# Differential attention: values projected two heads at a time straight into token rows

## The chip, the cores and the metric

The kernel runs on one core of a Trainium2 chip. The metric is the device time of one execution in microseconds (us), and the number to compare is the median of several runs. A core has five engines that work side by side, each with its own queue of instructions: PE (TensorE, matrix products; its weight loads are listed as PEld), DVE (VectorE), ACT (ScalarE), POOL (GpSimd) and SP (SyncE, which here issues most DMAs). Matmuls write into PSUM, a small memory of eight banks; the other operands live in SBUF. DMAs move data between SBUF and HBM.

## What is computed

The reference is an encoder trunk of two layers over 512 tokens of width 1024. In each layer the normalised input `h` goes through one wide projection `h @ w_in[l]`, whose columns feed three token mixers (MLA, windowed attention, differential attention) and three gates per channel; the merged result goes through `w_out`. The part that matters here is the differential attention: 4 heads, each with two score maps of dimension 64 and one value of dimension 128.

```
qc, kc, vc, zc = columns of h @ w_in[l]          # 512 columns each: 4 heads x 128
q, k = qc, kc as (S, 4 heads, 2, 64);  v = vc as (S, 4 heads, 128)
s = q . k / 8 + bias[head]                       # two maps per head, 512 x 512
p = softmax(s)
a = p[0] - lam * p[1]
o = rms_norm(a @ v, g_sub) * (1 - lam_init)
o_c = (o * silu(zc)) @ w_o_diff[l]
```

## The kernel before

**Precision by splitting.** A product of two float32 operands is made from three matmuls in the type fp32r: each operand is split into a high part (an ACT copy that rounds) and a low part (a DVE subtract), and `mm3` (lines 86 to 89) adds up high x high, high x low and low x high in one PSUM bank. The input of the layer is held transposed and split, in `hh` and `hl`: 128 channels in the partitions, 8 blocks `k` of channels, 512 tokens along the free dimension.

**Projections.** `wunit` (line 100) fetches a block of weights of 128 x 1024 elements (512 KB) into a buffer `wr` by a DMA on SP and splits it into `wh` (ACT, line 81) and `wl` (DVE, line 84). There are 2 buffers `wr` and 3 each of `wh` and `wl` (line 61). These steps have a high priority in the schedule, so they run ahead as far as buffers allow. `proj_T` (line 451) takes one unit, 128 columns with all 8 blocks `k`, and makes 24 matmuls: the weights are loaded into the array and the 512 tokens stream past. The result is 128 columns x 512 tokens, that is transposed, in a PSUM bank of the kind `dn`, of which there are 2. The other banks are `sc` (2, scores), `tr` (2, transposes), `av` (1) and `pj` (1).

**Order.** A scheduler lays out every engine's queue when the program is built. It takes the order of the program text as priority and lets later work start early where operands and buffers are ready. `tc.high_priority` moves a block forward. So independent projections fill TensorE while the softmax of a head runs on DVE, ACT and POOL.

**Differential attention** (line 924). `diff_qkv` (line 904) prepares a head: `stack_q` projects q, `proj_T` with `stack_k` projects k, and the value is projected by a third `proj_T`. The values are needed with tokens in the partitions, so `v_transposed` (line 805) copies the projection from PSUM to SBUF on ACT (buffer `tf`), transposes its four blocks of 128 x 128 on TensorE against the identity into the bank `pj` (line 810), and then ACT copies the high part (line 920) and DVE subtracts the low part (line 921) into a `big` buffer `vt` of 128 x 2 x 512. `first(hd)` makes the scores and the softmax of a head (lines 928 to 954). `second(hd, pr)` transposes the probabilities block by block (line 691) and multiplies them with the values (line 962), then normalises. The main loop (lines 982 to 996) prepares heads 0 and 1, starts `first(0)`, and then for each head runs: z's projection and its silu, one step of the merge of the windowed attention (`fill`), `first` of the next head, `second` of this head, and `diff_qkv` of the head after the next. `gates_late` and `gate_rows` (lines 505 and 280) follow behind the attention, then the merge of its output. `bg_step` advances unrelated work for later (modulation rows).

**The windowed attention** (line 839) matters as a comparison: its score matmuls (lines 865 and 866) stream 256 or 384 columns instead of 512. It uses `v_transposed` once a layer, too, and keeps it.

Of the kernel before, what the change touches and what calls it, by code (L numbers as in the profile page):

```python
# [12 lines left out]
F32R = mybir.dt.float32r  # L13
# [4 lines left out]
P = 128  # L18
S = 512
D = 1024  # L20
KT = D // P
NT = S // P
# [13 lines left out]
C_VC = 3232  # L36
# [14 lines left out]
def hybrid_kernel(ctx, tc, x, c, w_ada, b_ada, g_pre, g_post, w_in, g_q, w_uq, g_kv, w_ukv,  # L51
# [11 lines left out]
    def T(tag, shape, dt=F32, bufs=None):  # L63
        count[0] += 1
        return sb.tile(shape, dt, tag=tag, name=f"{tag}_{count[0]}",
                       bufs=bufs or BUFS.get(tag, 1))
# [6 lines left out]
    def Q(tag):  # L73
        count[0] += 1
        return ps.tile([P, S], F32, tag=tag, name=f"ps_{tag}_{count[0]}", bufs=PB[tag])

    def f(ap):
        return ap.bitcast(F32)

    def act_copy(out_, in_, scale=1.0):  # L80
        return act.activation(out=out_, in_=in_, func=AF.Copy, scale=scale)  # L81

    def sub(out_, a, b, eng=None):
        return (eng or dve).tensor_tensor(out=out_, in0=a, in1=b, op=ALU.subtract)  # L84

    def mm3(o, ah, al, bh, bl, start, stop):
        pe.matmul(o, ah, bh, start=start, stop=False)  # L87
        pe.matmul(o, ah, bl, start=False, stop=False)  # L88
        pe.matmul(o, al, bh, start=False, stop=stop)  # L89
# [3 lines left out]
    @contextmanager  # L93
    def behind(*ins):
        with ExitStack() as es:
            for i in ins or fence:
                es.enter_context(tc.issue_after(i.ins))
            yield

    def wunit(parts, big=False):  # L100
        raw = T("wr", [P, 1024])
        h = T("big" if big else "wh", [P, 1024], F32R)
        lw = T("big" if big else "wl", [P, 1024], F32R)
        n = parts[-1][1]
        with tc.high_priority(offset=WOFF[0]):
            for lo, hi, src, shp in parts:
                dst = raw[:, lo:hi]
                if shp:
                    dst = dst.rearrange("p (a b) -> p a b", a=shp)
                sp.dma_start(out=dst, in_=src)  # L110
            with behind():
                act_copy(h[:, :n], raw[:, :n])
                sub(lw[:, :n], raw[:, :n], f(h[:, :n]))
        return h, lw
# [160 lines left out]
    def bg_step(n=1):  # L275
        for _ in range(n):
            if bg and next(bg[0], bg) is bg:
                bg.clear()
# [172 lines left out]
    def proj_T(l, col, hh, hl):  # L451
        wh, wl = wunit([(0, 1024, w_in[l][:, col:col + P].rearrange("(k p) c -> p k c", p=P), KT)])
        acc = Q("dn")
        for k in range(KT):
            mm3(acc, wh[:, k * P:(k + 1) * P], wl[:, k * P:(k + 1) * P], hh[:, k], hl[:, k],
                k == 0, k == KT - 1)
        return acc
# [340 lines left out]
    def stack_k(src, i, kh):  # L798
        hi = slice(i * 64, i * 64 + 64)
        lo = slice(64 - i * 64, 128 - i * 64)  # L800
        act_copy(kh[hi], src[hi])
        dve.tensor_copy(out=kh[lo], in_=f(kh[hi]))
        return kh

    def v_transposed(vp):
        vf = T("tf", [P, S])
        act_copy(vf, vp)
        tr = Q("pj")
        for t in range(NT):
            pe.transpose(tr[:, t * P:(t + 1) * P], vf[:, t * P:(t + 1) * P], ident)  # L810
        return tr
# [89 lines left out]
        pipelined(first, second, 2 * NT)  # L901
        return o_all

    def diff_qkv(l, hd, hh, hl):
        bg_step()
        qq = stack_q(l, C_QC + hd * P, hh, hl)
        bg_step()
        kh = [T("op", [P, S], F32R) for _ in range(2)]
        kl = [T("op", [P, S], F32R) for _ in range(2)]
        ka = proj_T(l, C_KC + hd * P, hh, hl)  # L910
        for i in range(2):
            stack_k(ka, i, kh[i])
        for i in range(2):
            hi = slice(i * 64, i * 64 + 64)
            lo = slice(64 - i * 64, 128 - i * 64)
            sub(kl[i][hi], ka[hi], f(kh[i][hi]))
            dve.tensor_copy(out=kl[i][lo], in_=f(kl[i][hi]))
        vt = T("big", [P, 2, S], F32R)
        tr = v_transposed(proj_T(l, C_VC + hd * P, hh, hl))
        act_copy(vt[:, 0], tr)  # L920
        sub(vt[:, 1], tr, f(vt[:, 0]))
        return qq, kh, kl, vt

    def diff_attention(l, hh, hl, fill):
        o_all = []
        ops = {}

        def first(hd):
            qq, kh, kl, vt = ops[hd]
            b = T("x5", [P, 896])  # L930
            sp.dma_start(out=b, in_=skewed(bias_d[hd], 1023, 896))
            pr = T("p", [P, NT, S])
            for t in range(NT):
                ts_ = slice(t * P, (t + 1) * P)
                mx, nm, sm, rr = (stat(2) for _ in range(4))
                pc = [pr[:, t], T("ta", [P, S])]
                for i in range(2):
                    s = Q("sc")
                    pe.matmul(s, qq[i][:, ts_], kh[i], start=True, stop=False)  # L939
                    pe.matmul(s, qq[i][:, ts_], kl[i], start=False, stop=True)  # L940
                    dve.tensor_tensor_reduce(out=pc[i], in0=s, in1=b[:, 384 - t * P:896 - t * P],
                                             scale=1.0, scalar=-3.0e38, op0=ALU.add, op1=ALU.max,
                                             accum_out=mx[:, i:i + 1])
                    dve.tensor_scalar(out=nm[:, i:i + 1], in0=mx[:, i:i + 1], scalar1=-1.0,
                                      scalar2=None, op0=ALU.mult)
                    act.activation(out=pc[i], in_=pc[i], func=AF.Exp, bias=nm[:, i:i + 1],
                                   accum_out=sm[:, i:i + 1])
                dve.reciprocal(out=rr, in_=sm)
                dve.tensor_tensor(out=rr[:, 1:2], in0=rr[:, 1:2], in1=lam_neg[l], op=ALU.mult)  # L949
                pool.tensor_scalar(out=pc[1], in0=pc[1], scalar1=rr[:, 1:2], scalar2=1.0,  # L950
                                   op0=ALU.mult, op1=ALU.mult)
                dve.scalar_tensor_tensor(out=pc[0], in0=pc[0], scalar=rr[:, 0:1], in1=pc[1],
                                         op0=ALU.mult, op1=ALU.add)
            return pr

        def second(hd, pr):
            vt = ops[hd][3]
            av = Q("av")
            for kb in range(NT):
                ph, pl = transposed_block([pr[:, t, kb * P:(kb + 1) * P] for t in range(NT)])  # L960
                vs = slice(kb * P, (kb + 1) * P)
                mm3(av, vt[:, 0, vs], vt[:, 1, vs], ph, pl, kb == 0, kb == NT - 1)
            sq = T("ta", [P, S])
            sqh = T("pt", [P, S], F32R)
            sql = T("pt", [P, S], F32R)
            act.activation(out=sq, in_=av, func=AF.Square)
            act_copy(sqh, sq)
            sub(sql, sq, f(sqh))
            sq_ps = Q("pj")
            pe.matmul(sq_ps, onesr, sqh, start=True, stop=False)  # L970
            pe.matmul(sq_ps, onesr, sql, start=False, stop=True)
            rs = T("ta", [P, S])
            act.activation(out=rs, in_=sq_ps, func=AF.Ln, scale=1.0 / P, bias=epsc)
            act.activation(out=rs, in_=rs, func=AF.Exp, scale=-0.5)
            o = T("o", [P, S])
            dve.scalar_tensor_tensor(out=o, in0=av, scalar=gsub[l], in1=rs, op0=ALU.mult,
                                     op1=ALU.mult)
            dve.tensor_tensor(out=o, in0=o, in1=zc[hd], op=ALU.mult)
            o_all.append(split_u(o))

        zc = {}
        for hd in range(2):
            ops[hd] = diff_qkv(l, hd, hh, hl)
        with tc.high_priority(offset=20):
            pr = first(0)
        for hd in range(4):
            zc[hd] = silu_z(l, C_ZC + hd * P, hh, hl)
            fill(FN)
            if hd + 1 < 4:
                with tc.high_priority(offset=20):  # L990
                    nxt = first(hd + 1)
            with tc.high_priority(offset=20):
                second(hd, pr)
            pr = nxt
            if hd + 2 < 4:
                ops[hd + 2] = diff_qkv(l, hd + 2, hh, hl)
        return o_all

    def out_half(l, hf, mm):
# [126 lines left out]
    hh, hl, acc, za = layer0_input()  # L1126
    with behind(loads[-1]):
        setup_small()
    for l in range(DEPTH):
        if l > 0:  # L1130
            acc = acc4(True)
# [4 lines left out]
        hh, hl = new_hT() if l + 1 < DEPTH else (None, None)  # L1136
# [62 lines left out]
```

## Time and profile before

| | |
|---|---|
| median of 3 runs | 1209.92 us (1208.97 to 1210.29) |
| the profiled execution | 1208.57 us |
| its span, first to last instruction | 1206.8 us |
| mean granted TensorE clock | 0.993 |

The page of a profile gives, engine by engine, the busy time and share of the span, then the span in 40 equal slices with a digit for tenths busy. Groups of instructions read: line, engine, operation, output <- input by the program's names, shape, count, then busy time in us and the mean of one in ns, then the idle time of the engine just before them and what ended it. Timeline rows read: start in us, length in us, engine, line, operation, tiles, shape, and how many were merged into the row. A matmul's listed length includes the time in which the next one already runs, so lengths may overlap.

### The profile page before, as it was taken

How to read it: one execution, taken by the hardware profiler on the slowest of the kernel's cores; microseconds unless marked ns; L12 is line 12 of the kernel's file. 1: busy time of each engine (PE TensorE's matmuls, PEld its weight loads, DVE VectorE, ACT ScalarE, POOL GpSimd, SP SyncE). 2: the span in 40 equal slices, each digit the busy share in tenths (PEclk: the TensorE clock that was granted, in tenths of full speed). 3: DMA queues.
4: the chain of work that ended last, by engine and by line, in shares of the span. 5: the costliest groups of instructions: out<-in, count | busy, mean ns of one | idle time of the engine just before them, and what ended most of it. 6: DMA issues, size and time to landing. Idle time of an engine off the chain costs nothing.

```text
span 1206.8 us, 15578 instructions
## 1 busy us (share of the span) xinstructions
PE 1165.8 (97%) x5428; PEld 946.0 (78%) x5428; DVE 840.5 (70%) x1748; ACT 632.2 (52%) x1250; POOL 194.7 (16%) x238
## 2 busy tenths in 40 slices
PE   5799999999999999999999999999999999999997
PEld 4777788778887888887878888888888888888786
DVE  7854776988865687765557567678785468776553
ACT  5453565655543457654347456565554345665432
POOL 3410211111210010101141001122121001010123
PEclk9899999999999999999999999999999999999999
DMA  9638522356356333343454432324532432333442
GB/s 316 205 98 250 147 77 73 91 132 182 105 146 163 98 81 83 105 115 120 144 171 127 119 105 72 84 53 124 147 101 83 105 92 81 86 105 97 139 159 85
DMA packets 169523, 146.86 MB, mean 122 GB/s; under 512 B 7679, under 2 KB 146999, under 8 KB 169444
## 3 DMA queue, kind: packets, MB, share of 16 engines
q1 hardware_dynamic: 169316, 145.85, 41.9%
q8 instruction: 43, 0.70, 0.3%
q14 instruction: 36, 0.29, 0.1%
q0 software_dynamic: 128, 0.01, 0.0%
HBM read 135.83 MB, written 14.20 MB: 124 GB/s over the span
## 4 chain that ended last, share of the span: by engine, by line
PE 79%; DMA 7%; DVE 7%; issue 2%; POOL 2%; ACT 2%; SPq 1%; DVEq 0%; POOLq 0%; ACTq 0%
PE ps_dn L87 18%; PE ps_dn L89 18%; PE ps_dn L88 18%; PE ps_tr L691 5%; DMA wr<-in_w_in 3%; PE ps_sc L87 2%; PE ps_sc L89 2%; PE ps_sc L88 2%; PE ps_av L700 1%; PE ps_av L701 1%; PE ps_sc L939 1%; PE ps_sc L940 1%; DVE wl L84 1%; DMA wr<-in_w_ada 1%; PE ps_pj L87 1%
## 5 line engine op out<-in xcount | busy, mean ns | idle before, releaser
L87 PE MATMUL ps_dn<-hTh,wh 128*128 128x512 f32 x840 | 336.2, 400 | 1.7 <-ACT tf L479 1.1
L89 PE MATMUL ps_dn<-hTh,wl 128*128 128x512 f32 x840 | 334.5, 398 | 0.5 <-DVE wl L84 0.5
L88 PE MATMUL ps_dn<-hTl,wh 128*128 128x512 f32 x840 | 334.4, 398 | 0.0
L84 DVE TENSOR_TENSOR wl<-wr,wh 128x1024 fp32r<-128x1024 f32 x141 | 178.9, 1269 | 120.0 <-ACT wh L81 119.3
L81 ACT ACTIVATE wh<-wr 128x1024 fp32r<-128x1024 f32 x141 | 149.1, 1058 | 178.9 <-PE ps_dn L88 95.9
L87 PEld LDWEIGHTS ps_dn<-hTh,wh 128*128 128x128 f32 x840 | 158.1, 188 | 37.8 <-ACT tf L479 1.6
L89 PEld LDWEIGHTS ps_dn<-hTh,wl 128*128 128x128 f32 x840 | 157.9, 188 | 37.4 <-DVE wl L84 0.9
L88 PEld LDWEIGHTS ps_dn<-hTl,wh 128*128 128x128 f32 x840 | 158.0, 188 | 35.6
L84 DVE TENSOR_TENSOR pt<-ps_tr,pt 128x512 fp32r<-128x512 f32 x136 | 92.2, 684 | 35.2 <-ACT pt L81 34.4
L81 ACT ACTIVATE pt<-ps_tr 128x512 fp32r<-128x512 f32 x136 | 78.7, 596 | 70.8 <-PE ps_tr L691 69.5
L762 POOL TENSOR_SCALAR p<-p,st 128x512 f32<-128x512 f32 x64 | 48.6, 778 | 291.1 <-DVE st L760 237.6
L691 PE MATMUL ps_tr<-ident,p 128*128 128x128 f32 x544 | 93.0, 273 | 0.8 <-POOL p L762 0.8
L691 PEld LDWEIGHTS ps_tr<-ident,p 128*128 128x128 f32 x544 | 70.1, 141 | 20.7 <-POOL p L762 1.4
L87 PE MATMUL ps_dn<-u,wh 128*128 128x512 f32 x192 | 77.0, 401 | 1.3 <-DVE x L298 1.3
L950 POOL TENSOR_SCALAR ta<-ta,st 128x512 f32<-128x512 f32 x32 | 26.6, 833 | 313.9 <-DVE st L949 197.5
L89 PE MATMUL ps_dn<-u,wl 128*128 128x512 f32 x192 | 76.8, 400 | 0.0
L88 PE MATMUL ps_dn<-u,wh 128*128 128x512 f32 x192 | 76.1, 396 | 0.0
L881 POOL TENSOR_SCALAR p<-p,st 128x256 f32<-128x256 f32 (+1 forms) x64 | 41.4, 665 | 161.9 <-DVE st L879 116.0
L758 ACT ACTIVATE p<-ps_sc,st 128x512 f32<-128x512 f32 x64 | 43.7, 685 | 36.1 <-DVE st L757 35.9
L757 DVE TENSOR_REDUCE st<-ps_sc 128x1 f32<-128x512 f32 x64 | 43.3, 685 | 15.9 <-PE ps_sc L89 15.4
L873 ACT ACTIVATE p<-p,st 128x256 f32<-128x256 f32 (+1 forms) x64 | 35.6, 556 | 20.9 <-DVE st L871 20.2
L87 PEld LDWEIGHTS ps_dn<-u,wh 128*128 128x128 f32 x192 | 36.1, 188 | 10.4 <-DVE x L298 2.2
(345 smaller groups left out, 2105.0 us busy)
## 6 DMA issues: line engine op xcount, KB each, us to landing
wr<-in_w_in SPq DMA_DIRECT2D x105, 512.0 KB, 3.9
wr<-in_w_ada SPq DMA_DIRECT2D x32, 512.0 KB, 3.6
wr<-in_w_out SPq DMA_DIRECT2D x16, 512.0 KB, 3.7
big<-in_w_ada SPq DMA_DIRECT2D x10, 512.0 KB, 9.3
big<-in_x SPq DMA_DIRECT2D x8, 512.0 KB, 5.1
wr<-in_w_o_mla SPq DMA_DIRECT2D x8, 512.0 KB, 3.7
wr<-in_w_o_swa SPq DMA_DIRECT2D x8, 512.0 KB, 3.6
wr<-in_w_o_diff SPq DMA_DIRECT2D x8, 512.0 KB, 3.5
```

The source lines that it names most:

```text
L81: return act.activation(out=out_, in_=in_, func=AF.Copy, scale=scale)
L84: return (eng or dve).tensor_tensor(out=out_, in0=a, in1=b, op=ALU.subtract)
L87: pe.matmul(o, ah, bh, start=start, stop=False)
L88: pe.matmul(o, ah, bl, start=False, stop=False)
L89: pe.matmul(o, al, bh, start=False, stop=stop)
L691: pe.transpose(tr[:, i * P:(i + 1) * P], b, ident)
L757: dve.tensor_reduce(out=nm[:, t:t + 1], in_=s, axis=AX.X, op=ALU.max, negate=True)
L758: act.activation(out=pr[:, t], in_=s, func=AF.Exp, bias=nm[:, t:t + 1], accum_out=sm[:, t:t + 1])
L762: pool.tensor_scalar(out=pr[:, t], in0=pr[:, t], scalar1=rr[:, t:t + 1], scalar2=1.0, op0=ALU.mult, op1=ALU.mult)
L873: act.activation(out=pr[:, i, :w], in_=pr[:, i, :w], func=AF.Exp, bias=nm[:, i:i + 1], accum_out=sm[:, i:i + 1])
L881: pool.tensor_scalar(out=pr[:, i, :w], in0=pr[:, i, :w], scalar1=rr[:, i:i + 1], scalar2=1.0, op0=ALU.mult, op1=ALU.mult)
L950: pool.tensor_scalar(out=pc[1], in0=pc[1], scalar1=rr[:, 1:2], scalar2=1.0, op0=ALU.mult, op1=ALU.mult)
```

## The change

The value projection is taken out of `diff_qkv`, which becomes `diff_qk`. A new function `diff_v` makes the values of two heads in one go. It fetches two weight units, the first with blocks `k` 0 to 3 and the second with 4 to 7, each with the 256 value columns of both heads. The roles in the matmul are swapped: the input `hh`, `hl` is the operand that is loaded (128 channels x 128 tokens), and the 256 weight columns stream past. The result has tokens in the partitions. One `dn` bank takes two token blocks of 256 columns; there are two such banks a pair of heads, each with 2 x 8 x 3 = 48 matmuls. From a bank, for each of the two heads, ACT copies the high part and DVE subtracts the low part, 128 x 2 x 128 elements at a time, into the head's `vt`.

In the main loop, `diff_v` for heads 0 and 1 stands behind q and k of both heads and ahead of `first(0)`; that for heads 2 and 3 stands at the end of the round of head 1, behind q and k of head 3.

```diff
-    def diff_qkv(l, hd, hh, hl):
+    def diff_qk(l, hd, hh, hl):
...
-        vt = T("big", [P, 2, S], F32R)
-        tr = v_transposed(proj_T(l, C_VC + hd * P, hh, hl))
-        act_copy(vt[:, 0], tr)
-        sub(vt[:, 1], tr, f(vt[:, 0]))
-        return qq, kh, kl, vt
+        return qq, kh, kl
+
+    def diff_v(l, hd, hh, hl):
+        us = [wunit([(0, 1024, w_in[l][k * P:(k + 4) * P, C_VC + hd * P:C_VC + (hd + 2) * P]
+                      .rearrange("(k p) c -> p k c", p=P), 4)]) for k in (0, 4)]
+        vts = [T("big", [P, 2, S], F32R) for _ in range(2)]
+        for t2 in range(0, NT, 2):
+            acc = Q("dn")
+            for t in range(2):
+                ts_ = slice((t2 + t) * P, (t2 + t + 1) * P)
+                o = acc[:, t * 256:(t + 1) * 256]
+                for k in range(KT):
+                    wh, wl = us[k // 4]
+                    cs_ = slice((k % 4) * 256, (k % 4 + 1) * 256)
+                    mm3(o, hh[:, k, ts_], hl[:, k, ts_], wh[:, cs_], wl[:, cs_],
+                        k == 0, k == KT - 1)
+            av = acc.rearrange("p (t h b) -> p t h b", t=2, h=2)
+            for h in range(2):
+                vs = slice(t2 * P, (t2 + 2) * P)
+                vh = vts[h][:, 0, vs].rearrange("p (t b) -> p t b", t=2)
+                vl = vts[h][:, 1, vs].rearrange("p (t b) -> p t b", t=2)
+                act_copy(vh, av[:, :, h])
+                sub(vl, av[:, :, h], f(vh))
+        return vts
...
-            vt = ops[hd][3]
+            vt = vs_[hd]
...
+        vs_ = []
         for hd in range(2):
-            ops[hd] = diff_qkv(l, hd, hh, hl)
+            ops[hd] = diff_qk(l, hd, hh, hl)
+        vs_ += diff_v(l, 0, hh, hl)
...
             if hd + 2 < 4:
-                ops[hd + 2] = diff_qkv(l, hd + 2, hh, hl)
+                ops[hd + 2] = diff_qk(l, hd + 2, hh, hl)
+            if hd == 1:
+                vs_ += diff_v(l, 2, hh, hl)
```

More of the change, by code (lines that the diff above doesn't have):

```diff
@@ L928, in first @@
         def first(hd):
-            qq, kh, kl, vt = ops[hd]
+            qq, kh, kl = ops[hd]
             b = T("x5", [P, 896])
```

## The prediction

> **What bounds the kernel now.** I read the page first, parts 1, 2 and 4, and then only stretches of the trace around the projections.
>
> ```profile
> span 1206.8 us, 15578 instructions
> PE 1165.8 (97%) x5428; PEld 946.0 (78%) x5428; DVE 840.5 (70%) x1748; ACT 632.2 (52%) x1250; POOL 194.7 (16%) x238
> PE   5799999999999999999999999999999999999997
> PEclk9899999999999999999999999999999999999999
> PE 79%; DMA 7%; DVE 7%; issue 2%; POOL 2%; ACT 2%; SPq 1%; DVEq 0%; POOLq 0%; ACTq 0%
> ```
>
> TensorE is busy in nine tenths or more of every slice from the third to the last but one, at full granted clock, and the chain that ended last is 79% TensorE. A busy share alone could still hide slow matmuls, so the stages that the change touches come next: their windows (one per layer), and who TensorE waited for in each of them.
>
> ```profile
> 380.00:550.00 170.00, 169.62 (x771) 136.73 (x770) 123.41 (x261) 97.13 (x163) 13.33 (x16) 1.00 0.38 107
> 950.00:1125.00 175.00, 175.00 (x795) 141.47 (x794) 124.56 (x263) 101.83 (x170) 13.32 (x16) 1.00 0.36 100
> PE ps_dn L87 <- DVE op L794: 0.4, 1, 0.4
> PE ps_dn L292 <- DVE x L298: 0.8, 1, 0.8
> ```
>
> The columns are the window, its length, then busy time of PE, PEld, DVE, ACT and POOL, the clock, the DMA share and GB/s. In the differential attention TensorE is idle for 0.4 us of 170 and for nothing of 175. Its only wait inside the head loop is 0.4 us on L794; the one on L298 belongs to the gate rows behind it. So the time of this stage is the number of matmuls times the distance from one start to the next. Busy time isn't that distance, since matmuls overlap: it has to be read from starts in the timeline.
>
> **The change, part by part.** First the distance of the 512-wide matmuls, in a stretch of nothing else:
>
> ```profile
> 546.20 0.39 PE L88 MATMUL ps_dn<-hTl,wh 128*128 128x512 f32 x1
> ...
> 554.84 0.40 PE L89 MATMUL ps_dn<-hTh,wl 128*128 128x512 f32 x1
> ```
>
> There are 37 intervals between these two starts: 8.64 / 37 = 0.2335 us each, although each is shown as 0.39 long. A value projection of one head (L919) is 24 of them: 24 x 0.2335 = 5.60 us.
>
> Then the transposes that go (four a head, L810):
>
> ```profile
> L810 PE MATMUL ps_pj<-ident,tf x16: 270/272/273, 401.4 to 493.7; 128*128 128x128 f32 x16
> 401.12 0.40 PE L89 MATMUL ps_dn<-hTh,wl 128*128 128x512 f32 x1
> 401.35 0.60 PE L810 MATMUL ps_pj<-ident,tf 128*128 128x128 f32 x4
> 401.70 0.48 PE L87 MATMUL ps_dn<-hTh,wh 128*128 128x512 f32 x1
> 402.02 0.40 PE L88 MATMUL ps_dn<-hTl,wh 128*128 128x512 f32 x1
> ```
>
> From 401.12 to 402.02 are 0.90 us. Two 512-wide matmuls in it are worth 0.467, so four transposes cost 0.43 us, 0.11 each; I take 0.44, the length that four times 0.11 gives. Each is listed as 0.272 long, but the next one starts after 0.11. Before: 5.60 + 0.44 = 6.04 us a head.
>
> Now the matmuls that come: 4 token blocks x 8 k x 3 for two heads, 48 a head, each 256 wide. The trace has that shape in the windowed attention, where q and k are the operands:
>
> ```profile
> 307.10 0.28 PE L865 MATMUL ps_sc<-op,op 128*128 128x256 f32 x1
> ...
> 307.58 0.27 PE L691 MATMUL ps_tr<-ident,p 128*128 128x128 f32 x1
> 826.74 0.28 PE L865 MATMUL ps_sc<-op,op 128*128 128x256 f32 x1
> ...
> 827.20 0.39 PE L701 MATMUL ps_av<-pt,big 128*64 128x512 f32 x1
> 872.90 0.28 PE L865 MATMUL ps_sc<-op,op 128*128 128x256 f32 x1
> ...
> 873.37 0.40 PE L88 MATMUL ps_dn<-hTl,wh 128*128 128x512 f32 x1
> ```
>
> Each pair of rows spans four 256-wide matmuls in a row: 0.48, 0.46 and 0.47 us, so 0.120, 0.115 and 0.1175 us each. I take 0.1175, the middle: half of 0.2335 would be 0.1168, so the price is per column and splitting a pass costs hardly anything. After: 48 x 0.1175 = 5.64 us a head.
>
> The sum for TensorE is 5.64 - 6.04 = -0.40 us a head, times 8 heads (4 in each of 2 layers) = **-3.2 us**. With 0.115 it is -0.52 x 8 = -4.2, with 0.120 it is (5.76 - 6.04) x 8 = -2.2. The whole gain is the transposes; the projection itself stays level.
>
> Runs of four are the longest that the trace has, and the new passes are 48 long, so wider bounds stand behind this. The weights of each matmul are loaded separately, and the transposes, which stream only 128 columns, show how fast loads can follow each other: 0.11. From below, 48 x 0.11 = 5.28, -0.76 x 8 = -6.1 us. From above, a load that did not overlap the stream would make 0.11 + 0.1175 = 0.2275: 48 x 0.2275 = 10.92, +4.88 x 8 = +39 us. The quadruples are nearest by far, since they are the same instruction with a load before each.
>
> The Trainium skill speaks for that upper bound: "TensorE: Matmul & The Clock Gate", Part 3 (Packing small matmuls — row/col tiling), says that a weight load overlaps a matmul in flight only when they are in different row groups. All loads here use all rows. The trace disagrees with it: loads and streams of full-height matmuls run 0.1175 apart, which leaves no place for 0.11 of load outside. The rule's result is rival A below.
>
> The copies. Per pair of heads, the ACT copy of the projection (tf), the ACT copy of the transposed values and the DVE subtract, each 512 wide and twice, become 4 ACT copies and 4 DVE subtracts, 256 wide:
>
> ```profile
> L81 ACT ACTIVATE tf<-ps_dn 128x512 f32<-128x512 f32 x10 | 5.9, 589 | 0.1
> L81 ACT ACTIVATE big<-ps_pj 128x512 fp32r<-128x512 f32 x10 | 5.9, 589 | 3.6 <-PE ps_pj L810 3.6
> L84 DVE TENSOR_TENSOR big<-ps_pj,big 128x512 fp32r<-128x512 f32 x10 | 6.8, 684 | 0.1
> L599 ACT ACTIVATE ta<-ps_sc 128x256 f32<-128x256 f32 x4 | 1.5, 378 | 0.1
> L867 DVE CUSTOM_DVE_ANT_0 p<-ps_sc,x,sinkt 128x256 f32<-128x256 f32 x32 | 14.2, 477 | 5.0 <-PE ps_sc L866 4.1 <-PE ps_tr L691 0.9
> ```
>
> ACT: 4 x 0.589 = 2.36 to 4 x 0.378 = 1.51 us a pair; DVE: 2 x 0.684 = 1.37 to at most 4 x 0.477 = 1.91. Both lie beside TensorE's work (ACT is busy 97 of 170 us in the stage, DVE 123), and I cost them at nothing. What they can hold up is a dn buffer: with copies and subtracts in two pairs it is free about 1.3 us after the last matmul (0.378 + 0.378 + 0.477) instead of 0.59. The other dn buffer takes a pass of 48 x 0.1175 = 5.6 us meanwhile; without that cover it would cost 0.7 us for each of 8 buffers, 5.6 us.
>
> The weights. Before, 8 loads of 512 KB, one unit a head; now 8 loads again, two units a pair. But both units stay in use through all 11.3 us of a pass, two of the three wh/wl buffers, and the second is wanted 12 matmuls (1.4 us) after the first.
>
> ```profile
> wr<-in_w_in SPq DMA_DIRECT2D x18, 512.0 KB, 3.9
> wr<-in_w_o_swa SPq DMA_DIRECT2D x4, 512.0 KB, 3.7
> L81 ACT ACTIVATE wh<-wr 128x1024 fp32r<-128x1024 f32 x141 | 149.1, 1058 | 178.9 <-PE ps_dn L88 95.9 <-DMA wr<-in_w_in 41.0 <-issue 21.8
> L84 DVE TENSOR_TENSOR wl<-wr,wh 128x1024 fp32r<-128x1024 f32 x141 | 178.9, 1269 | 120.0 <-ACT wh L81 119.3
> ACT wh L81 <- PE ps_dn L88: 19.6, 12, 4.4
> ```
>
> The new units have 1 KB rows in HBM, as those of w_o_swa have, instead of 512 B, and should land in 3.7 us rather than 3.9; I reckon with 3.9. A unit needs that to land and 1.06 + 1.27 = 2.3 to be split, and lasts 5.6. The splits already wait for buffers (the last row: 19.6 us in 12 waits in the first layer's stage), that is, weights are ahead of TensorE. The second unit's buffer comes free when k of the second head begins, 5.6 us before the pass: split in time. The unit behind the pass has the third buffer, and covers the split of the next with its own 5.6 us. I cost this at nothing. If the cover is gone, only the split is late (2.3 - 1.4 = 0.9 us a pass) or the load too (3.9 + 2.3 - 1.4 = 4.8); that is rival B. What queues behind a split that waits on ACT are the exponentials (L946), and for those wait DVE's L952 and the transposes of the head; other projections fill TensorE meanwhile.
>
> The move. The value work of head 2, 6.0 us of TensorE with its load on SP, goes from before z of head 1 to behind k of head 3, past the loads of z, q and k; nothing of it is on POOL. (That of head 0 goes behind q and k of head 1 in the same way, with no attention of these heads in between; that of head 3 stays.) It was cover for the softmax of head 1; what takes its place is the z, merge step, q and k that stood behind it. The last chain has slack, too:
>
> ```profile
> 551.07 0.69 DVE L84 TENSOR_TENSOR u<-o,u 128x512 fp32r<-128x512 f32 x1 [0.70 <-ACT u L81]
> 555.07 0.39 PE L292 MATMUL ps_dn<-pt,onesr 128*128 128x512 f32 x1
> ```
>
> The last head's result is split at 551.8, and TensorE has projections until 555.1: 3.3 us of slack against 1.6 us a layer that it loses. So the whole gain should arrive.
>
> **Sum.** The profiled execution took 1208.57 us (span 1206.8 and 1.8 around it). It lies 1.35 below the median of the runs, 1209.92. 1208.57 - 3.2 = 1205.4; on the median, 1206.7, which is what I predict.
>
> **Rivals.** A: loads don't hide behind the short stream, +39 us as above, 1249. Against it stand the rows of four; for it, only that no long run is shown. 0.03.
>
> B, the other side: the second weight unit comes late at each of the four passes, because two of three buffers are taken. It costs 0.9 to 4.8 us a pass. At 0.9 the sum is +0.4, 1210; at 4.8 it is +16, 1226. It decides at (3.2 + 2.4) / 4 = 1.4 us a pass, from where the kernel is slower by more than 0.2%. For it: ACT waited 7.3 us for loads in the stage.
>
> ```profile
> ACT wh L81 <- DMA wr<-in_w_in: 7.3, 2, 4.5
> ```
>
> Against it: TensorE didn't wait at all then. 0.12 for the costly part.
>
> C: the transposes cost what they are listed as. 32 x 0.272 = 8.7 us go and 0.04 x 8 = 0.3 come: -8.4, 1201.5. The Trainium skill, in "TensorE: Matmul & The Clock Gate", Part 4 (PE-mode transpose), gives about 275 ns for one within a kernel; the trace agrees on the length and not on the spacing. Chance 0.04.
>
> D: no change, within 2.4 us. TensorE saves its 3.2 but the new order of work puts 1 to 3 us of waits where there are almost none (head 1's softmax with less cover, a dn buffer late): 1209. 0.26.
>
> **How the numbers follow.** The forecast has 0.55. Measurements of this kernel tell about 0.2% (2.4 us) from no change, so the forecast's -3.2 is only just beyond; of its own range (-4.2 to -2.2) a small part lies within. Faster 0.53 (forecast without that part 0.49, C 0.04), same 0.32 (D 0.26, the forecast's edge 0.06), slower 0.15 (A 0.03, B 0.12). The range goes from 1203.5 (just below the bound of 6.1) to 1212, which takes in D and the cheap part of B and leaves out A, C and the dear part of B. The forecast's own range is 1205.7 to 1207.7.
>
> **What would show it.** In the profile after: no L810 but the 8 of the windowed attention; 384 matmuls of 128x256 into ps_dn, starts 0.1175 apart over a pass; PE idle in the two stages still under 1 us each; no wait of PE for wl or wh at the start of a pass. A spacing of 0.126 (6.04 / 48) would make the change worth nothing, 0.132 a loss of 0.2%. Gaps of over 1 us in front of the 13th matmul of a pass would be B.

## The result, and the profile after

| | before | changed |
|---|---|---|
| median of 20 runs | 1210.24 us | 1213.58 us |
| ratio to before, 95% interval | | 1.0025 [1.0018, 1.0032] |
| the profiled execution's span | 1206.8 us | 1210.1 us |
| mean granted TensorE clock | 0.993 | 0.988 |

The kernel became slower by 0.25% (3.0 us by the ratio, 3.3 us by the medians), where 3.2 us less was forecast; the median lies outside the range of 1203.5 to 1212. The page of the changed kernel, parts 1 and 2:

```profile
span 1210.1 us, 15903 instructions
PE 1169.3 (97%) x5588; PEld 956.4 (79%) x5588; DVE 841.8 (70%) x1756; ACT 626.8 (52%) x1250; POOL 192.4 (16%) x238
PE   5899999999998999999999999999999999999997
PEclk9899999989999999999999999999999999999999
```

There are 160 more matmuls: 384 came, and 192 of 512 columns and 32 transposes went. A tenth is missing in the 13th slice, around 380 us, where the first layer's differential attention begins. The windows of the two stages and TensorE's waits in them, in the columns used before:

```profile
380.00:550.00 170.00, 166.42 (x836) 137.96 (x836) 122.63 (x265) 95.90 (x166) 12.44 (x16) 0.99 0.36 101
950.00:1125.00 175.00, 174.55 (x878) 145.03 (x877) 124.22 (x267) 98.50 (x170) 12.44 (x16) 1.00 0.35 96
PE ps_dn L87 <- DVE op L794: 3.1, 1, 3.1
PE ps_av L88 <- DVE pt L84: 0.5, 1, 0.5
```

TensorE was idle for 0.4 us in the first layer's stage before and is now idle for 3.6; in the second layer it goes from 0 to 0.45. The wait on L794 was there before with 0.4 us and now has 3.1. The one on `pt` is new and comes once a layer.

First the term on which the forecast rested. A whole value bank without anything between, first matmul of the bank and the one behind its last:

```profile
412.79 0.28 PE L87 MATMUL ps_dn<-wh,hTh 128*128 128x256 f32 x1
...
418.45 0.40 PE L87 MATMUL ps_dn<-hTh,wh 128*128 128x512 f32 x1
L84 DVE TENSOR_TENSOR big<-ps_dn,big 128x256 fp32r<-128x256 f32 x16 | 6.7, 417 | 0.0
L81 ACT ACTIVATE big<-ps_dn 128x256 fp32r<-128x256 f32 x16 | 6.0, 373 | 8.6 <-DVE big L84 5.5 <-PE ps_dn L89 3.1
```

48 intervals take 5.66 us, 0.118 each; 0.1175 was forecast. The copies take 0.373 and 0.417 us, 0.378 and at most 0.477 were reckoned. So the work on TensorE did shrink by 8 x (6.04 - 5.66) = 3.0 us. The time went elsewhere, to the place where the page shows the missing tenth. PE in the changed kernel around 390 us:

```profile
389.16 0.40 PE L89 MATMUL ps_dn<-hTh,wl 128*128 128x512 f32 x1
392.69 0.47 PE L87 MATMUL ps_dn<-hTh,wh 128*128 128x512 f32 x1 [3.13 <-DVE op L794]
...
393.83 0.63 PE L88 MATMUL ps_dn<-hTl,wh 128*128 128x512 f32 x1
394.26 0.63 PE L89 MATMUL ps_dn<-hTh,wl 128*128 128x512 f32 x1
...
397.11 0.39 PE L87 MATMUL ps_dn<-hTh,wh 128*128 128x512 f32 x1
```

The start at 392.69 comes 3.53 us after the one before, 3.3 late. Then matmuls from 393.83 on start 0.43 apart instead of 0.2335, up to 396.82: TensorE runs at about half its clock. In all, the 13 intervals from 389.16 to 397.11 take 7.95 us in place of 13 x 0.2335 = 3.04: 4.9 us are lost, 3.3 in the gap and 1.6 behind it. That is more than the gain.

What TensorE waits for there is a bank. It has finished q of head 0 (its last matmul starts at 383.56) and k of head 0 (389.16) in the two `dn` banks, and the next projection needs q's bank emptied. ACT's and DVE's rows in the changed kernel:

```profile
381.94 1.06 ACT L81 ACTIVATE wh<-wr 128x1024 fp32r<-128x1024 f32 x1 [4.00 <-DMA wr<-in_w_in]
...
388.16 1.06 ACT L81 ACTIVATE wh<-wr 128x1024 fp32r<-128x1024 f32 x1 [4.12 <-DMA wr<-in_w_in]
389.13 0.57 ACT L81 ACTIVATE op<-ps_dn 64x512 fp32r<-64x512 f32 x1
389.25 1.23 DVE L84 TENSOR_TENSOR wl<-wr,wh 128x1024 fp32r<-128x1024 f32 x1 [2.60 <-ACT wh L81]
390.51 0.68 DVE L794 SCALAR_TENSOR_TENSOR op<-ps_dn,op 64x512 fp32r<-64x512 f32 x1
391.23 0.59 ACT L81 ACTIVATE op<-ps_dn 64x512 fp32r<-64x512 f32 x1 [1.53 <-DVE op L794]
391.85 0.69 DVE L794 SCALAR_TENSOR_TENSOR op<-ps_dn,op 64x512 fp32r<-64x512 f32 x1 [0.66 <-ACT op L81]
```

The two copies that empty q's bank (`op<-ps_dn`) stand in ACT's queue behind the split of a later weight unit, that of k of head 1. That split waits for its load until 388.16. On DVE the other half of the same split (L84 at 389.25) stands ahead of the first L794 and holds it until 390.51, 0.8 us after the copy that it needs (389.13 + 0.57). Before the change, the split in this place is that of q of head 1, which was the fourth unit of its sequence as k of head 1 is now:

```profile
384.38 1.06 ACT L81 ACTIVATE wh<-wr 128x1024 fp32r<-128x1024 f32 x1 [4.45 <-DMA wr<-in_w_in]
385.35 0.57 ACT L81 ACTIVATE op<-ps_dn 64x512 fp32r<-64x512 f32 x1
```

ACT was blocked for 4.45 us then, too, but 3.8 us earlier; TensorE felt the last 0.4 of it. Why the load of the fourth unit comes later now (issued at 384.29, before at 380.44) stands in SP's queue, before the change and after it (start, length of the issue with its wait):

```profile
371.03 1.51 SPq L110 DMA_DIRECT2D wr<-in_w_in  x2
377.50 0.34 SPq L225 DMA_DIRECT2D wr<-in_w_ada  x1
380.44 0.37 SPq L110 DMA_DIRECT2D wr<-in_w_in  x1
```

```profile
370.85 0.38 SPq L110 DMA_DIRECT2D wr<-in_w_in  x1
371.99 0.33 SPq L225 DMA_DIRECT2D wr<-in_w_ada  x1
377.83 0.38 SPq L110 DMA_DIRECT2D wr<-in_w_in  x1
378.26 0.57 SPq L528 DMA_DIRECT2D tf<-gb  x1
378.96 0.34 SPq L225 DMA_DIRECT2D wr<-in_w_ada  x1
380.81 0.33 SPq L528 DMA_DIRECT2D tf<-gb  x1
384.29 6.59 SPq L110 DMA_DIRECT2D wr<-in_w_in  x3
```

`diff_qk` still makes its two background steps, and each loads a block of `w_ada` into one of the two `wr` buffers. The value unit of head 0 used to stand between those of head 0 and those of head 1. Taken out, every unit is followed by a `w_ada` load: the sequence was k, v, ada, q, ada, k and is k, ada, q, ada, k. With one of two buffers lent to `w_ada`, a load waits for the split of the last unit: that of k of head 1 is issued at 384.29, when DVE has done the low part of q's unit (383.03 + 1.23). A second thing moved as well: the value copies into `tf` are gone, so that the gate loads into `tf` (L528) come early and stand in the same place. That made two theories.

The second layer of the same profile already tells between them. It has the new order of units and gate loads among them (L528 at 950.50 and 959.27), but no `w_ada` load any more: the last issue on L225 is at 880.5. There the split waits for a buffer and not for a load, the copy of q follows at once, and TensorE has no wait on L794.

```profile
963.48 1.06 ACT L81 ACTIVATE wh<-wr 128x1024 fp32r<-128x1024 f32 x1 [3.50 <-PE ps_dn L88]
964.44 0.57 ACT L81 ACTIVATE op<-ps_dn 64x512 fp32r<-64x512 f32 x1
```

### The profile page after: what moved, and what is told of

The parts are those of the page before. It is cut to its first block, busy times and chain, and to the rows that moved or that the text cites. A ratio compares the mean times of both kernels' runs of the same rounds, so it can differ in the third digit from the quotient of the medians.

```text
span 1210.1 us, 15903 instructions
## 1 busy us (share of the span) xinstructions
PE 1169.3 (97%) x5588; PEld 956.4 (79%) x5588; DVE 841.8 (70%) x1756; ACT 626.8 (52%) x1250; POOL 192.4 (16%) x238
## 4 chain that ended last, share of the span: by engine, by line
PE 77%; DMA 8%; DVE 7%; issue 2%; ACT 2%; POOL 2%; SPq 1%; DVEq 0%; POOLq 0%; ACTq 0%
PE ps_dn L87 18%; PE ps_dn L88 18%; PE ps_dn L89 18%; PE ps_tr L691 5%; DMA wr<-in_w_in 2%; PE ps_sc L87 2%; PE ps_sc L89 2%; PE ps_sc L88 2%; PE ps_av L700 1%; PE ps_av L701 1%; DVE wl L84 1%; PE ps_sc L959 1%; PE ps_sc L958 1%; DMA wr<-in_w_ada 1%; PE ps_av L88 1%
## 5 line engine op out<-in xcount | busy, mean ns | idle before, releaser
L87 PE MATMUL ps_dn<-hTh,wh 128*128 128x512 f32 x776 | 312.5, 403 | 5.5 <-DVE op L794 3.1
L89 PE MATMUL ps_dn<-hTh,wl 128*128 128x512 f32 x776 | 310.1, 400 | 0.5 <-DVE wl L84 0.5
L88 PE MATMUL ps_dn<-hTl,wh 128*128 128x512 f32 x776 | 310.2, 400 | 0.0
L84 DVE TENSOR_TENSOR wl<-wr,wh 128x1024 fp32r<-128x1024 f32 x141 | 178.1, 1264 | 119.4 <-ACT wh L81 118.4
L87 PEld LDWEIGHTS ps_dn<-hTh,wh 128*128 128x128 f32 x776 | 146.8, 189 | 38.4 <-issue 3.5
L89 PEld LDWEIGHTS ps_dn<-hTh,wl 128*128 128x128 f32 x776 | 146.7, 189 | 34.7 <-DVE wl L84 0.9
L88 PEld LDWEIGHTS ps_dn<-hTl,wh 128*128 128x128 f32 x776 | 146.7, 189 | 32.4
L84 DVE TENSOR_TENSOR pt<-ps_tr,pt 128x512 fp32r<-128x512 f32 x136 | 91.9, 685 | 22.2 <-ACT pt L81 21.2
L965 ACT ACTIVATE p<-p,st 128x512 f32<-128x512 f32 x32 | 23.1, 722 | 45.0 <-DVE st L963 45.0
```

## The experiments

All ratios are to the kernel before, in the same set of runs. Theory 1: the `w_ada` loads next to each unit, and ACT's queue behind the late one. Theory 2: the gate loads.

**Loads moved behind.** The two background steps of head 1 go into the value pass.

```diff
     def diff_qk(l, hd, hh, hl):
-        bg_step()
+        bg_step(hd != 1)
         qq = stack_q(l, C_QC + hd * P, hh, hl)
-        bg_step()
+        bg_step(hd != 1)
...
         vts = [T("big", [P, 2, S], F32R) for _ in range(2)]
+        bg_step(2 * (hd == 0))
```

> The changed kernel, with the two background steps of head 1 (each loads 512 KB of w_ada into a wr buffer) moved from the projections of q and k of head 1 to the value pass of heads 0 and 1, so that the w_ada loads no longer stand between the weight units. Theory 1 (taking the value unit of head 0 out of the sequence put the w_ada loads next to every unit; a unit arrives one load later, ACT's queue stands at its split, q's bank isn't emptied): the 3.1 us wait of TensorE at 389 us on L794 goes, with it the half clock behind it, 1.7 us, and the kernel comes to 1213.5 - 4.4 = about 1209. Theory 2 (the gate loads into tf, which the removed copies used to keep out, come early and delay the weights; they stay as in the changed kernel): the wait stays, 1213.

Measured: 0.9985 [0.9976, 0.9994], 1208.2 us. The wait is gone, as theory 1 says; the gate loads still stand among the units (L528 at 373.67 and 380.40), so theory 2 falls.

**Old values in the new place.** The value pass for two heads, but made as before the change.

```diff
     def diff_v(l, hd, hh, hl):
...
+        vts = []
+        for h in range(hd, hd + 2):
+            vt = T("big", [P, 2, S], F32R)
+            tr = v_transposed(proj_T(l, C_VC + h * P, hh, hl))
+            act_copy(vt[:, 0], tr)
+            sub(vt[:, 1], tr, f(vt[:, 0]))
+            vts.append(vt)
         return vts
```

> The kernel before, with its old value projection (512 wide, with transposes) done for two heads at the places where the change does it. This has the new order without the new shape, and the gate loads into tf stay late because the copies into tf are still there. Theory 1: the wait at 389 us is there with the old shape too, 3 us and 1.7 us of half clock: 1210.2 + 4.3 = about 1214.5. Theory 2: no such wait, 1210.

Measured: 1.0043 [1.0030, 1.0056], with a wait of 3.3 us on L794. The old shape in the new order is slower than before by 5 us: the loss needs no 256-wide matmul. It needs no early gate load either, since none is issued here before the wait ends.

**Old values, new place, loads behind.** The two edits together.

> The old value projection (512 wide, with transposes) at the places where the change does it, with the two background steps of head 1 moved behind the weight units of q and k. With the kernel of old values at the new place (1.0043) and the two of new values (1.0025 and 0.9985) it makes a table of two by two: shape against order of loads. Theory 1: the order of loads is worth 4 to 5 us with either shape, so this comes to before or 0.6 us under it, 1.000, and new values stand 2 to 3 us under old ones in both rows. If the shape itself cost something (a split pass of 11 us, bank held longer), this would be as fast as new values with the loads behind, 0.9985, or faster.

Measured: 1.0000 [0.9991, 1.0009]. With the runs above:

| | loads between the units | loads behind |
|---|---|---|
| old values, new place | 1.0043 | 1.0000 |
| new values, new place | 1.0025 | 0.9985 |

Down a column the shape gains 0.18% and 0.15%, 2.2 and 1.8 us; along a row the order of loads is worth 0.43% and 0.40%, about 5 us. By the intervals, each of these differences is known to about 0.15%, so the gain of the shape is only just clear of nothing. That it is under the 3.0 us of work fits the waits: both kernels with new values have the wait on `pt` in each layer, and those with old values have a shorter one there instead (0.3 to 0.4 us, on the scores).

**One split moved.** Theory 1 has two steps, and the one on ACT can be tried alone: the split of k's unit of head 1 is put behind the copies that empty q's bank of head 0. No load changes its place.

```diff
+            qe = [act_copy(q[hi], src[hi], 0.125),
+                  dve.scalar_tensor_tensor(out=q[lo], in0=src[hi], scalar=0.125, in1=f(q[hi]),
+                                           op0=ALU.mult, op1=ALU.subtract)]
+        qend.append(qe)
...
+        if l == 0 and hd == 1:
+            fence[:] = qend[-2]
         ka = proj_T(l, C_KC + hd * P, hh, hl)
+        fence.clear()
```

> The changed kernel with a single step moved on ACT and its partner on DVE: the split of the unit of k of head 1 (layer 0) stands behind the two copies that empty q's bank of head 0, instead of in front of them. All loads keep their order, and that unit still lands at about 388 us. If the wait at 389 us is the place in ACT's queue (q's copies stand behind a split that waits for its load), it goes or is under 0.6 us, with it the half clock, and the kernel comes to about 1209 (1213.5 - 4.4). If the late weights themselves are what TensorE lacks (or w_ada's use of the DMA), the wait stays, some 3 us on wh or wl instead of L794, and the time stays at 1213.5.

Measured: 0.9989 [0.9979, 0.9998], 1208.81 us. ACT in this kernel:

```profile
385.21 0.59 ACT L81 ACTIVATE op<-ps_dn 64x512 fp32r<-64x512 f32 x1 [0.20 <-PE ps_dn L89]
388.37 0.59 ACT L81 ACTIVATE op<-ps_dn 64x512 fp32r<-64x512 f32 x1 [2.57 <-DVE op L794]
389.38 1.06 ACT L81 ACTIVATE wh<-wr 128x1024 fp32r<-128x1024 f32 x1 [0.41 <-DMA wr<-in_w_in]
```

The unit is split no sooner than before the edit (389.38 against 388.16), and nobody misses it. Only the copies are earlier, and the 3.1 us and the half clock are gone. From 1.0025 to 0.9989 are 0.36%, 4.4 us, what was expected. So TensorE wasn't short of weights; it was kept from an empty bank by the place of one split in the queues of ACT and DVE. The edit moves both halves of the split, so the share of each queue isn't shown apart.

**Value pass behind k of head 0.**

```diff
             ops[hd] = diff_qk(l, hd, hh, hl)
-        vs_ += diff_v(l, 0, hh, hl)
+            if hd == 0:
+                vs_ += diff_v(l, 0, hh, hl)
```

> The changed kernel, with the value pass of heads 0 and 1 placed right behind q and k of head 0, where the value of head 0 stood before; the sequence of loads is then unit, w_ada, unit, unit, unit, w_ada, as before the change. Theory 1: the wait at 389 us goes or is under 0.6 us as before the change, no half clock, about 1209. Theory 2: gate loads into tf still stand among the units here, so the wait stays, 1213.

Measured: 1.0055 [1.0039, 1.0071]. The wait at 389 us is gone as expected, and the time is wrong by 6 us. TensorE's idle time moved: 3.0 us in the first stage and 2.0 in the second.

```profile
380.00:550.00 170.00, 167.00 (x842) 137.45 (x841) 120.99 (x262) 94.87 (x163) 13.10 (x16) 1.00 0.37 105
950.00:1125.00 175.00, 173.00 (x864) 142.79 (x863) 122.51 (x265) 95.64 (x166) 13.10 (x16) 0.99 0.35 96
```

They are several waits of about 1 us, in both layers at the scores of the fourth head (L958) and behind a silu (L466). In the second layer half clock follows them: 512-wide matmuls start 0.43 apart from 1076.43 to 1078.14. Why that order has these waits wasn't followed.

**Values of heads 2 and 3 a round earlier.** This is for the second, smaller wait, that on `pt`.

```diff
-            if hd == 1:
+            if hd == 0:
                 vs_ += diff_v(l, 2, hh, hl)
```

> The changed kernel, with the value pass of heads 2 and 3 at the end of the round of head 0, where the value of head 2 stood before, instead of head 1. It tells whether the wait of 0.6 us in each layer (TensorE on the last low part of the probabilities of head 1, at 471 and 1046 us) comes from the missing filler in the round of head 0. If so it goes, 2 x 0.7 = 1.4 us: 1212. The wait at 389 us stays under both theories. If the place doesn't matter: 1213.5.

Measured: 1.0021 [1.0012, 1.0030]. The wait on `pt` is gone from both layers, the one on L794 is 3.8 us. The step in time from 1.0025 lies within the intervals. The rows of the changed kernel show the wait itself:

```profile
470.06 0.68 DVE L794 SCALAR_TENSOR_TENSOR op<-ps_dn,op 64x512 fp32r<-64x512 f32 x1
470.77 0.75 DVE L971 SCALAR_TENSOR_TENSOR p<-p,st,ta 128x512 f32<-128x512 f32 x1
471.44 0.15 DVE L963 TENSOR_SCALAR st<-st 128x1 f32<-128x1 f32 x1
471.50 0.68 DVE L84 TENSOR_TENSOR pt<-ps_tr,pt 128x512 fp32r<-128x512 f32 x1
```

The low part of head 1's probabilities (L84 at 471.50) stands behind the eviction of q of head 3 (L794), which comes early since no value of head 2 is projected ahead of it. With the value pass a round earlier, the same eviction starts at 486.0, and the wait is gone.

**Both moves.** The background steps behind, and heads 2 and 3 a round earlier.

> The changed kernel with both moves: the two background steps of head 1 in the value pass of heads 0 and 1, and the value pass of heads 2 and 3 at the end of the round of head 0. If the two waits are separate causes, both go, and what is left is the 3.1 us of TensorE work: before - 3.1, with the 0.6 us that the kernel before itself waits on L794 perhaps 0.6 more; about 0.997 of before. If one move only shifts the wait elsewhere, the time stays at that of the first move alone, 0.9985.

Measured: 0.9974 [0.9961, 0.9987], 1206.49 us against 1209.86. Its stages:

```profile
380.00:550.00 170.00, 170.00 (x861) 141.70 (x860) 124.21 (x265) 94.94 (x165) 11.47 (x16) 1.00 0.38 108
950.00:1125.00 175.00, 175.00 (x882) 145.93 (x881) 125.23 (x266) 99.33 (x170) 11.47 (x16) 1.00 0.35 99
```

TensorE is idle for nothing in either stage. This version is faster than the kernel before and the changed one. Against before it gains 3.1 us (1.6 to 4.7 by the interval), close to the prediction's sum; that it is so close is in part luck, since the 0.4 us that the kernel before waits on L794 went too.

## Why the prediction was wrong

- **The terms on TensorE were right.** 5.66 us a head measured, 5.64 forecast; 3.0 us of work gone, 3.2 forecast. Rival A (loads that don't hide) is refuted by banks of 48 at 0.118. Rival C, by which the transposes cost their listed lengths, 8.4 us in all, is refuted by the table: the new shape gains 2.2 and 1.8 us.
- **The copies and the bank were right.** No wait stands on a value bank. (The working has a slip: 0.378 + 0.378 + 0.477 is 1.23, not 1.3. Nothing hangs on it.)
- **The weights of the value pass were right in what they say, and rival B didn't come.** TensorE didn't wait for wl or wh at the start of a pass.
- **The step that failed is "The move", with "I cost this at nothing" for the weights ahead of it.** From this the time of the stage was to be the number of matmuls times their distance, with no wait; the runs show a wait of 3.1 us on L794 in its place, 4.9 us lost with the half clock. The step counted what moves (the value units, 8 loads before and 8 after) and not what stays: the two background steps, each a load of 512 KB into the same two buffers, between which a value unit went missing. The prediction named which loads head 2's value passes on SP, and dismissed head 0's, with no attention in between, in a bracket; that bracket is where the 4.9 us arose. It looked for the price on TensorE's side, as lost cover; what there was of that, the wait on `pt`, costs 0.6 us a layer.
- **A sign was quoted and not read.** The 0.4 us on L794 was called the only wait inside the head loop. Followed to ACT, it shows a queue blocked for 4.45 us on a load, with less than no slack: a load that came 3 us later in this place would be paid in full. The same 4.45 us are in the 7.3 that rival B quotes, and its answer there, that TensorE didn't wait at all then, is wrong: behind them stand the 0.4 us. One step back along that wait could have changed the forecast.
- **Rival D had the mechanism in outline,** waits from the new order, "a dn buffer late", but sized them at 1 to 3 us. They measure 4.9 us here, half clock included, against 0.6 before the change in the same stretch, and 0.6 once a layer on `pt`. -3.0 + 4.3 + 1.2 = +2.5 of the 3.3 by which the two profiled spans differ.
- **Stage by stage it fits.** From the last matmul of k of head 0 to the first gate row (L292 at 555.07, now 558.68) the first layer takes 3.3 us more, where -1.5 + 4.3 + 0.6 = 3.4 was to come. From the first L865 row of the second layer (826.74, now 831.03) to its first gate row (1130.17, now 1133.67) it takes 0.8 less, where -1.5 + 0.6 = -0.9 was to come. The rest lies outside: 0.3 ahead of these stages and 0.7 between them, less 0.1 behind. Between them the program is the same in all nine kernels, and their profiles scatter there from 271.7 to 273.0 us, so nothing is read into it.

## What to carry to other kernels

When work is taken out of a sequence, list what its neighbours share with it, buffers and queues above all, and look at what now stands side by side. An in-order queue that waits for a load holds back everything behind it: if one of those instructions empties a bank that the bound engine needs, the load is on the critical path though no weight is missing. A wait of a few tenths of a us on the bound engine is the end of a slack; follow it back before calling the rest of the stage free.

## What the runs showed of the hardware

A wait of 3 to 4 us on TensorE costs half as much again or more: the granted clock falls for a while after work has resumed. Windows from 380 to 400 us of four kernels, in this order: the changed one, old values in the new place, the one with the split moved, and the one with both moves. The clock is the figure behind POOL.

```profile
380.00:400.00 20.00, 16.87 (x66) 13.17 (x66) 11.26 (x16) 6.55 (x10) 0.00 (x0) 0.91 0.59 175
```

```profile
380.00:400.00 20.00, 16.74 (x61) 13.00 (x60) 10.79 (x15) 6.47 (x9) 0.00 (x0) 0.83 0.52 141
```

```profile
380.00:400.00 20.00, 20.00 (x88) 16.04 (x87) 14.28 (x20) 8.85 (x12) 0.00 (x0) 1.00 0.65 186
```

```profile
380.00:400.00 20.00, 20.00 (x88) 16.04 (x87) 12.59 (x18) 7.64 (x11) 0.00 (x0) 1.00 0.49 135
```

The two with the wait (3.1 and 3.3 us) are at 0.91 and 0.83 over these 20 us, the two without it at 1.00. The kernel with a wait of 3.8 us is at 0.83, too. In the changed kernel the loss behind the gap is 1.6 us. With the old values in the new place half clock lasts longer: the 16 intervals from 388.50 to 398.49 take 9.99 us in place of 3.74, of which 3.4 are the gap and 2.8 the loss behind it.

The Trainium skill, "TensorE: Matmul & The Clock Gate", section "Part 1: The HAM clock gate (the "warmup" mystery)", has the clock halve after an idle window of about 3.4 us and asks to keep gaps under that. Half clock agrees (0.43 against 0.2335 us a matmul); the length doesn't quite, since 3.13 us idle were enough here. The kernel before has a shorter gap with half clock behind it, in the first layer's windowed attention; its 512-wide matmuls start 0.43 apart from 256.63 to 257.91:

```profile
255.40 0.69 PE L865 MATMUL ps_sc<-op,op 128*128 128x384 f32 x1 [2.70 <-DVE st L867]
```

Ahead of that gap TensorE runs short matmuls of one and of 128 columns, so what its length alone does isn't shown. Nor does one length settle it: with the value pass behind k of head 0, the same waits of about 1 us at the fourth head are followed by half clock in the second layer and not in the first.
